# S5 preparation and scans in PSUM rings of their own, with second buffers and another order of parts

## The chip, the cores and the metric

The kernel runs on one core of one Trainium2 chip. The metric is the device time of one execution in microseconds (us). The engines are TensorE (PE; its weight loads are PEld), VectorE (DVE), ScalarE (ACT), GpSimd (POOL) and SyncE (SP), which issues all the transfers.

## The reference

One layer of a decoder trunk with two groups of heads, for 1024 new positions and 8 single tokens, in float32:

```
proj = x @ w_in                                   # q, k, v, z, two logits, u
q, k, v = short_conv(proj[qkv]);  o, S = gated_delta_chunked(q, k, v, g, beta, s0)
bu = b_bar * u;  bu[0] += lam_bar * h0            # S5: 32 groups of 16 channels, 64 complex states each
_, h = associative_scan(combine, (lam_bar, bu))   # combine = (a1*a2, a2*b1 + b2)
ys = real(c @ h) + d_skip * u
ys = gelu(ys);  ys = ys * sigmoid(ys @ w_glu + b_glu)
x = layernorm(alpha*x + concat(o, ys) @ w_out)
x = layernorm(alpha*x + relu(x @ w_ff1)**2 @ w_ff2)
```

## The kernel before

All dense products are split in a high and a low part and take three matmuls each (hi*hi, hi*lo, lo*hi). A tile of the input projection (`conv_tile`, `u_tile`) has 128 output columns: 8 slices of the 1024 inputs, three blocks of 344 positions, three matmuls each, 72 in all; its weights are loaded in two halves (`load_w`), cast by ACT (`whi`, L110) and the rest taken by POOL (`wlo`, L111). A conv tile is then evicted by ACT (L292), scaled by ACT (L300), gets three steps of the short convolution on DVE (L302) and a Silu on ACT (L303).

`run` starts with the first two u tiles beside the loads of x, then runs a list of steps, `S5O`: `uN` is a u tile, `qN`, `kN`, `vN` are conv tiles of head N, `sN` is part N of S5 (four groups of channels), `e0` the final states. Then the mixers follow, with the preparation of the GDN heads first (`gdn_prep`: transposes at L332 and L341, squares on ACT at L335, products at L357 and L358, DVE's L361 and L375). The tile framework's scheduler orders the instructions of the steps on each engine by their dependences; only from the mixers on is the order of PE written by hand.

A part of S5 (`s5_part`) has a preparation and two scans. The preparation loads `bc4`, makes small products (L925 to L932), two tables (`table`: DVE L941, POOL L942, DVE L943), of which `nat` is transposed on PE (L950) and copied to `T1` by ACT, and `V1` feeds the kt matmuls (L958); `kt` goes to the Toeplitz matrix `MT` by eight transfers (L963). Phases give `cs` and `sn` (L966 to L973). Then the carries of two pairs of groups are made by PE (L984, tile `h1`). Each pair is scanned: copies by ACT (L994), rotation by DVE (L996 to L998), two scans (L1003), copies (L1006), back rotation into `H` (L1007 to L1009). The outputs `y` are matmuls with `MT` (L1015) and `V1` (L1016); ACT copies them to `ge` (L1018), and SP stores them (L1020). `U`, `MT` and `H` have two buffers each.

PSUM has eight banks. `psum(mm, sm, ch)` opens rings of that many banks: `mmps()` takes from the first, `psm()` from the second, `pch()` from the third. In the S5 stage there are two for dense tiles and six for everything else:

```python
self.psum(2, 6)
BC, BT, BG, B3, B5 = (1, 1, 1, 2, 4)   # buffers of cs and sn, of T1, of ge; B5: of the scratch tiles t5
```

A part takes twelve banks from the ring of six, in this order: the small products, `nat`, the transposes, `V1`, kt, the phases, two `h1`, then for each pair the work bank `sb_` and `y`.

Of the kernel before, what the change touches and what calls it, by code (L numbers as in the profile page):

```python
# [11 lines left out]
AF = mybir.ActivationFunctionType  # L12
OP = mybir.AluOpType
# [12 lines left out]
RING = "XXLLLLLLQBQBQBQBQBQBQBQQCQCQQB"  # L26
FORMS = {"B11": "QL", "B21": "QL", "B12": "XX", "B22": "CL", "T1": "BQ", "T2": "BQ", "T3": "BQ", "T4": "BQ"}
TO = 2
# [18 lines left out]

LW = ((2.5, 8.25, 3.0), (3.0, 8.25, 3.0), (3.0, 8.25, 2.0), (3.0, 12.25, 3.5))
TS, MW, MF = (2, 19, 0.3)
S5O = "s0 u2 q0 s1 s2 k0 v0 u3 s3 q1 k1 v1 s4 s5 q2 k2 v2 s6 s7 e0 q3 k3"  # L50
BC, BT, BG, B3, B5 = (1, 1, 1, 2, 4)
WB = 6
WX = 1
TE = (0, 1, 2, 3)
# [4 lines left out]
class Kernel:  # L59
# [838 lines left out]
    def s5_part(self, t, du):  # L898
        nc = self.nc
# [5 lines left out]
        sb = lambda name, shape, bufs=1: sp.tile(shape, F32, name=name, tag=name, bufs=bufs)  # L905
# [11 lines left out]
        B, iB, C0, iC = (bc4[:, :, i, :] for i in range(4))  # L917
        dsk = sb("dsk", [16, 4, 16], 2)
        nc.sync.dma_start(dsk, self.a["dsk"][:, gs, :])
        tb = self.psm()[:, :128].rearrange("p (k g c) -> p k g c", g=4, c=16)  # L920
        pBb, pC0 = (tb[:, k] for k in range(2))
        Bb, iBb = sb("Bb", [128, 4, 16], 2), sb("iBb", [128, 4, 16], 2)
        w1, w2 = sb("bw1", [128, 4, 16]), sb("bw2", [128, 4, 16])
# [10 lines left out]
        sh = [128, 4, 8, 16]  # L934
        col = lambda z, a, b: z[:, gs, a:b, None].to_broadcast([128, 4, b - a, 16])
        bc = lambda z: z[:, :, None, :].to_broadcast(sh)
        bank = lambda: self.psm().rearrange("p (g k c) -> p g k c", k=8, c=16)

        def table(out, a, x, b, y, op):
            p, tm = bank(), sb("t5", sh, B5)  # L940
            V.tensor_tensor(p, a, bc(x), op=OP.mult)  # L941
            G.tensor_tensor(tm, b, bc(y), op=OP.mult)  # L942
            V.tensor_tensor(out, p, tm, op=op)  # L943

        nat = sb("t5", sh, B5)
        table(nat, col(self.prev[0], 0, 8), pBb, col(self.prev[1], 0, 8), iBb, OP.add)
        T1 = sb("T1", [128, 4, 128], BT)
        p = self.psm().rearrange("p (g m) -> p g m", m=128)
        for g in range(4):
            nc.tensor.transpose(p[:, g, :], nat[:, g].rearrange("p k c -> p (k c)"), self.ident)  # L950
        nc.scalar.activation(T1, p, AF.Copy)
        V1 = sb("V1", [128, 4, 9, 16], 2)
        nc.scalar.activation(V1[:, :, 0, :], C0, AF.Copy, scale=self.nsgn)
        table(V1[:, :, 1:9, :], col(self.lrn, 0, 8), pC0, col(self.lpi, 1, 9), iC, OP.subtract)
        kt = sp.tile([16, 4, 128], F32, name="kt", tag="t5", bufs=B5)
        p = self.psm()[:16].rearrange("p (g m) -> p g m", m=128)
        for g in range(4):
            nc.tensor.matmul(p[:, g, :], Bb[:, g, :], V1[:, g, 0:8, :].rearrange("p k c -> p (k c)"),  # L958
                             start=True, stop=True)
# [5 lines left out]
        cs3, sn3 = sb("cs", sh, BC), sb("sn", sh, BC)  # L965
        ph = sb("t5", sh, B5)  # L966
        G.tensor_tensor(ph, self.steps[:, None, :].to_broadcast(sh), self.c8[:, gs, None].to_broadcast(sh), op=OP.mult)
        p = self.psm().rearrange("p (g m) -> p g m", m=128)
        nc.scalar.activation(p, ph, AF.Identity, bias=self.magic)
        V.scalar_tensor_tensor(ph, p, -MAGIC, ph, op0=OP.add, op1=OP.subtract)  # L970
        nc.scalar.activation(sn3, ph, AF.Sin, scale=self.turn)
# [8 lines left out]
        for j in range(2):  # L980
            h1 = self.psm()
            hin.append(h1)
            for i in range(2):
                nc.tensor.matmul(h1[:, 136 * i:136 * i + 136], T1[:, 2 * j + i, :], U[:, 2 * j + i, 0:136],  # L984
                                 start=True, stop=True)
        for j in range(2):
            pr = slice(2 * j, 2 * j + 2)
            gp = slice(g0 + 2 * j, g0 + 2 * j + 2)
            h1 = hin[j][:, :272].rearrange("p (g m) -> p g m", m=136)
            sb_ = self.psm()  # L990
            sw, b = r3(sb_[:, 0:256]), r3(sb_[:, 256:512])
            b1 = sb("s5b1", [128, 2, 128], 2)
            for o, z in ((top, bot), (bot, top)):
                nc.scalar.activation(sw[o], h1[z, :, 8:136], AF.Copy)  # L994
            nc.scalar.activation(self.hinS[:, gp, :], h1[:, :, 0:8], AF.Copy)
            V.tensor_tensor(b1, h1[:, :, 8:136], cs3[:, pr, :], op=OP.mult)  # L996
            V.tensor_tensor(sw, sw, sn3[:, pr, :], op=OP.mult)
            V.tensor_tensor(b, b1, sw, op=OP.subtract)  # L998
            H = self.H[j]
            b2 = r3(hin[j][:, 0:256])  # L1000
            for i in range(2):
                g = g0 + 2 * j + i
                V.tensor_tensor_scan(b2[:, i, :], self.rho[:, g:g + 1].to_broadcast([128, 128]), b[:, i, :], 0.0,  # L1003
                                     op0=OP.mult, op1=OP.add)
            for o, z in ((top, bot), (bot, top)):
                nc.scalar.activation(sw[o], b2[z], AF.Copy)  # L1006
            V.tensor_tensor(H[:, :, 1:128], b2[:, :, 0:127], cs3[:, pr, 0:127], op=OP.mult)  # L1007
            V.tensor_tensor(sw[:, :, 0:127], sw[:, :, 0:127], sn3[:, pr, 0:127], op=OP.mult)
            V.tensor_tensor(H[:, :, 1:128], H[:, :, 1:128], sw[:, :, 0:127], op=OP.add)  # L1009
            nc.scalar.activation(self.glast[:, gp], b2[:, :, 127], AF.Copy)  # L1010
            nc.scalar.activation(H[:, :, 128:136], self.h0[:, gp, :], AF.Copy)
            y = self.psm()[:, :272].rearrange("p (g m) -> p g m", m=136)
            for i in range(2):
                g = 2 * j + i
                nc.tensor.matmul(y[:, i, :], MT[:, g, :], U[:, g, 8:144], start=True, stop=False)  # L1015
                nc.tensor.matmul(y[:, i, :], V1[:, g, 1:9, :].rearrange("p k c -> p (k c)"), H[:, i, :],  # L1016
                                 start=False, stop=True)
            nc.scalar.activation(ge[:, pr, :], y, AF.Copy)  # L1018
# [134 lines left out]
    def t_forms(self, acc, c):  # L1153
        nc = self.nc
        V, G = nc.vector, nc.gpsimd
        h = [slice(HN * j + CH * c, HN * j + CH * c + CH) for j in range(2)]
        F = {t: self.form(t, c) for t in ("T1", "T2", "T3", "T4")}
        for i in range(4):
# [3 lines left out]
            V.tensor_tensor(t[0], a12, a11, op=OP.subtract)  # L1162
            self.split_b(t[0], F["T1"][i], None, i in TP[0])
            V.tensor_tensor(t[1], a22, t[0], op=OP.subtract)
# [78 lines left out]
    def run(self):  # L1243
        nc, tc = self.nc, self.tc
# [15 lines left out]
        w = [[None, None] for _ in range(2)]  # L1260
        units = []
        w[0][0] = self.load_w(self.a["win"][16][:, 0:512])
        self.load_x(0)
        self.lam = [self._s5c(z, [128, 32], z) for z in ("aim", "ldt", "are")]
        self.lam = [self.lam[i] for i in (2, 0, 1)]
        self.setup_ba()
        w[1][0] = self.load_w(self.a["win"][17][:, 0:512])
        for k in (1, 2, 3):
            self.load_x(k)
        w[0][1] = self.load_w(self.a["win"][16][:, 512:1024])  # L1270
# [18 lines left out]
        dus = self.u_evac((0, 1), units)  # L1289
        self.ba(pss)  # L1290
        qkv = {h: [] for h in range(4)}
        self.psum(2, 6)
        for step in S5O.split():
            t = int(step[1:])
            if step[0] == "s":
# [127 lines left out]
    def bank(self):  # L1423
        return self.sb.tile([128, 1024], F32, name="sb", tag="sb")
# [28 lines left out]
    def pair(self, p):  # L1453
# [40 lines left out]
        T = bank()  # L1494
        product(T, "T1", self.form_w(s1), True)
        m5 = copy(T)
# [406 lines left out]
```

## Time and profile before

| | us |
|---|---|
| median of 3 runs | 1309.6 (1309.11 to 1309.62) |
| the profiled execution | 1303.56 |
| its span, first to last instruction | 1301.8 |
| PE busy | 1218.3 (94%) |
| DVE busy | 846.7 (65%) |
| ACT busy | 638.3 (49%) |
| POOL busy | 556.5 (43%) |

1.8 us of the profiled execution lie outside its span. Times in the trace count from the start of the span. Matmuls overlap, so that a matmul's own duration is about twice the distance from one start to the next; where work on PE is added up, distances between starts are used. The granted clock of PE is 1.00 at 2.4 GHz and 0.50 at 1.2 GHz. The S5 stage reaches from about 45 us to 256 us.

### The profile page before, as it was taken

What the parts mean: (1) busy time and instruction counts of PE and PEld (TensorE: products, weight loads), DVE (VectorE), ACT (ScalarE), POOL (GpSimd) and SP (SyncE); (2) the same over time, 40 slices, a digit from 0 to 9 for tenths busy, and PEclk for the clock granted to TensorE, in tenths of its full rate; (3) what the DMA queues carried; (4) which work ended last, traced back from release to release, by engine and by line L of the source; (5) the groups of instructions that cost most, each with busy time, mean ns of one, the idle gap of its engine ahead of it and who ended that gap; (6) DMA issues with size and microseconds to landing.
All of it is one profiled execution on the core that took longest, in us unless ns stands there. A gap on an engine that the chain in (4) does not pass through costs nothing.

```text
span 1301.8 us, 24910 instructions
## 1 busy us (share of the span) xinstructions
PE 1218.3 (94%) x9268; PEld 1186.4 (91%) x9268; DVE 846.7 (65%) x1720; ACT 638.3 (49%) x1458; POOL 556.5 (43%) x564
## 2 busy tenths in 40 slices
PE   8999998598999999989999999999899899998996
PEld 7999998488989899978999999999889898998995
DVE  6466777598546885777832323232997978778678
ACT  5366666473456752347755555555443333333200
POOL 6223343162204661544533332333657953476224
PEclk8999999599979899989999999999999999999998
DMA  7323222113441154013432232323544423334112
GB/s 213 110 58 93 65 66 80 33 16 104 131 144 34 56 171 141 1 37 115 126 123 100 105 107 98 120 100 110 164 155 126 149 91 117 121 99 155 64 40 92
DMA packets 96249, 131.14 MB, mean 101 GB/s; under 512 B 28776, under 2 KB 63992, under 8 KB 96128
## 3 DMA queue, kind: packets, MB, share of 16 engines
q1 hardware_dynamic: 96128, 129.55, 31.7%
q8 instruction: 73, 1.20, 0.4%
q14 instruction: 48, 0.39, 0.1%
HBM read 97.14 MB, written 31.20 MB: 99 GB/s over the span
## 4 chain that ended last, share of the span: by engine, by line
PE 67%; DVE 16%; issue 5%; DMA 5%; POOL 4%; ACT 3%; SPq 1%; POOLq 0%; DVEq 0%; ACTq 0%
PE sb L1438 29%; PE mm L153 7%; PE mm L155 7%; PE mm L154 7%; DMA hraw<-hd 3%; DVE t L111 2%; DVE wlo L111 1%; POOL wlo L111 1%; PE mm L1718 1%; DVE xB L1151 1%; POOL t L111 1%; PE mm L1720 1%; PE mm L1719 1%; DVE acc L1137 1%; PE mm L140 1%
## 5 line engine op out<-in xcount | busy, mean ns | idle before, releaser
L111 POOL TENSOR_TENSOR wlo<-wraw,whi 128x512 fp32r<-128x512 f32 (+1 forms) x103 | 129.5, 1260 | 174.9 <-ACT whi L110 150.7
L110 ACT ACTIVATE whi<-wraw 128x512 fp32r<-128x512 f32 (+2 forms) x194 | 113.0, 583 | 160.7 <-PE sb L1438 100.8
L1438 PE MATMUL sb<-t,whi 128*128 128x258 f32 x1008 | 163.6, 285 | 8.8 <-DVE acc L1672 8.2
L1438 PEld LDWEIGHTS sb<-t,whi 128*128 128x128 f32 x1008 | 139.8, 191 | 10.4 <-DVE acc L1672 7.0
L1438 PE MATMUL sb<-xT,whi 128*128 128x258 f32 x832 | 133.8, 283 | 0.0
L153 PE MATMUL mm<-xhi,whi 128*128 128x344 f32 x384 | 127.1, 331 | 5.2 <-DVE zt L320 4.7
L154 PE MATMUL mm<-xlo,whi 128*128 128x344 f32 x384 | 124.5, 324 | 0.0
L155 PE MATMUL mm<-xhi,wlo 128*128 128x344 f32 x384 | 124.4, 324 | 0.0
L111 DVE TENSOR_TENSOR wlo<-wraw,whi 128x512 fp32r<-128x512 f32 (+2 forms) x91 | 68.6, 755 | 71.2 <-ACT whi L110 71.1
L1438 PEld LDWEIGHTS sb<-xT,whi 128*128 128x128 f32 x832 | 114.3, 189 | 0.0
L1438 PE MATMUL sb<-t,wlo 128*128 128x258 f32 x504 | 101.5, 285 | 2.7 <-POOL wlo L111 2.2
L1438 PE MATMUL sb<-xB,whi 128*128 128x258 f32 x624 | 100.3, 283 | 0.0
L1672 DVE TENSOR_TENSOR acc<-acc,sb 128x516 f32<-128x516 f32 x112 | 75.7, 684 | 34.6 <-PE sb L1438 34.3
L1438 PEld LDWEIGHTS sb<-xB,whi 128*128 128x128 f32 x624 | 85.9, 190 | 0.0
L1438 PE MATMUL sb<-xT,wlo 128*128 128x258 f32 x416 | 83.7, 283 | 0.0
L1438 PEld LDWEIGHTS sb<-t,wlo 128*128 128x128 f32 x504 | 78.2, 190 | 3.8 <-POOL wlo L111 3.0
L153 PEld LDWEIGHTS mm<-xhi,whi 128*128 128x128 f32 x384 | 72.9, 190 | 7.3 <-DVE zt L320 5.2
L1481 DVE TENSOR_TENSOR hst<-sb,hst 128x516 f32<-128x516 f32 x40 | 27.7, 695 | 76.0 <-PE sb L1438 75.9
L155 PEld LDWEIGHTS mm<-xhi,wlo 128*128 128x128 f32 x384 | 72.9, 190 | 0.2 <-issue 0.2
L154 PEld LDWEIGHTS mm<-xlo,whi 128*128 128x128 f32 x384 | 73.0, 190 | 0.0
L1438 PEld LDWEIGHTS sb<-xT,wlo 128*128 128x128 f32 x416 | 64.1, 188 | 0.0
L1438 PE MATMUL sb<-xB,wlo 128*128 128x258 f32 x312 | 63.1, 284 | 0.0
(517 smaller groups left out, 3571.1 us busy)
## 6 DMA issues: line engine op xcount, KB each, us to landing
hraw<-hd SPq DMA_DIRECT2D x44, 516.0 KB
hd<-hst SPq DMA_DIRECT2D x52, 258.0 KB
wpair<-in_wff SPq DMA_DIRECT2D x26, 512.0 KB
w2raw<-in_wff SPq DMA_DIRECT2D x64, 192.0 KB
wraw<-in_win SPq DMA_DIRECT2D x40, 256.0 KB
wraw<-in_wff SPq DMA_DIRECT2D x24, 256.0 KB
xr<-in_xT SPq DMA_DIRECT2D x24, 172.0 KB
wraw<-in_wout SPq DMA_DIRECT2D x16, 256.0 KB
```

The lines of the kernel that those rows point to most:

```text
L110: nc.scalar.activation(hi, src, AF.Copy)
L111: (lo_eng or nc.vector).tensor_tensor(lo, src, hi.bitcast(F32), op=OP.subtract)
L140: nc.tensor.matmul(ps, hi[:, k % 4, :], mh, start=(k == 0), stop=False)
L153: nc.tensor.matmul(ps, hi[:, k % 4, :], mh, start=(k == 0), stop=False)
L154: nc.tensor.matmul(ps, hi[:, k % 4, :], ml, start=False, stop=False)
L155: nc.tensor.matmul(ps, lo[:, k % 4, :], mh, start=False, stop=(k == last))
L1137: V.scalar_tensor_tensor(x, x, self.lnp[:, 0, i:i + 1], rb, op0=OP.mult, op1=OP.mult)
L1151: nc.vector.scalar_tensor_tensor(lo, x, b, hi.bitcast(F32), op0=OP.add, op1=OP.subtract)
L1438: self.nc.tensor.matmul(ps[:, 512 * c:512 * c + CH], a[:, k, :], forms[c][k][b], start=(start and k == 0 and a is hi and b == 0), stop=(st ...
L1481: V.tensor_tensor(h3, self.banks(ps), h3, op=OP.add)
L1672: V.tensor_tensor(a, a, self.banks(ps), op=OP.add)
L1718: nc.tensor.matmul(ps, hi[:, k % 4, :], mh, start=(k == 0), stop=False)
```

## The change

In the S5 stage PSUM gets three rings: two banks for dense tiles, three for preparation (`pch`), three for scans (`psm`). The preparation's six banks come from `pch`. In the scans `y` has no bank of its own but is written into the work bank `sb_` of its pair, so that a part takes four banks from the ring of three: two `h1`, then `sb_` of each pair. `cs`, `sn`, `T1` and `ge` get a second buffer. In the code of a part the table `V1` is made ahead of the transposes of `nat`. The list of steps is another, and at the program's start the small weights `wba` and a weight load are issued ahead of three small loads. No arithmetic changes.

```diff
-S5O = "s0 u2 q0 s1 s2 k0 v0 u3 s3 q1 k1 v1 s4 s5 q2 k2 v2 s6 s7 e0 q3 k3"
-BC, BT, BG, B3, B5 = (1, 1, 1, 2, 4)
+S5O = "s0 u2 s1 q0 u3 s2 k0 s3 v0 q1 s4 k1 s5 v1 q2 s6 k2 s7 v2 e0 q3 k3"
+BC, BT, BG, B3, B5 = (2, 2, 2, 2, 4)
...
-        tb = self.psm()[:, :128].rearrange("p (k g c) -> p k g c", g=4, c=16)
+        tb = self.pch()[:, :128].rearrange("p (k g c) -> p k g c", g=4, c=16)
...
-        bank = lambda: self.psm().rearrange("p (g k c) -> p g k c", k=8, c=16)
+        bank = lambda: self.pch().rearrange("p (g k c) -> p g k c", k=8, c=16)
...
+        V1 = sb("V1", [128, 4, 9, 16], 2)
+        nc.scalar.activation(V1[:, :, 0, :], C0, AF.Copy, scale=self.nsgn)
+        table(V1[:, :, 1:9, :], col(self.lrn, 0, 8), pC0, col(self.lpi, 1, 9), iC, OP.subtract)
         T1 = sb("T1", [128, 4, 128], BT)
-        p = self.psm().rearrange("p (g m) -> p g m", m=128)
+        p = self.pch().rearrange("p (g m) -> p g m", m=128)
...
-        V1 = sb("V1", [128, 4, 9, 16], 2)
-        nc.scalar.activation(V1[:, :, 0, :], C0, AF.Copy, scale=self.nsgn)
-        table(V1[:, :, 1:9, :], col(self.lrn, 0, 8), pC0, col(self.lpi, 1, 9), iC, OP.subtract)
         kt = sp.tile([16, 4, 128], F32, name="kt", tag="t5", bufs=B5)
-        p = self.psm()[:16].rearrange("p (g m) -> p g m", m=128)
+        p = self.pch()[:16].rearrange("p (g m) -> p g m", m=128)
...
-        p = self.psm().rearrange("p (g m) -> p g m", m=128)
+        p = self.pch().rearrange("p (g m) -> p g m", m=128)
         nc.scalar.activation(p, ph, AF.Identity, bias=self.magic)
...
-            y = self.psm()[:, :272].rearrange("p (g m) -> p g m", m=136)
+            y = sb_[:, :272].rearrange("p (g m) -> p g m", m=136)
...
+        self.setup_ba()
+        w[1][0] = self.load_w(self.a["win"][17][:, 0:512])
         self.lam = [self._s5c(z, [128, 32], z) for z in ("aim", "ldt", "are")]
         self.lam = [self.lam[i] for i in (2, 0, 1)]
-        self.setup_ba()
-        w[1][0] = self.load_w(self.a["win"][17][:, 0:512])
...
-        self.psum(2, 6)
+        self.psum(2, 3, 3)
```

At the end of the S5 stage PE has, before the change, these rows one behind the other. `ps_2593` and `ps_2596` are the carries of part 6, `ps_2616` and `ps_2639` its outputs, `ps_2722` and `ps_2745` the first carry and outputs of part 7, `pc_3035` the first transposes of the GDN preparation:

```order
L984 MATMUL ps_2596<-U0_359,T1_2550 128x136 x2
L1015 MATMUL ps_2616<-U0_359,MT0_357 128x136
...
L1016 MATMUL ps_2639<-H1_356,V1_2557 128x136
L958 MATMUL ps_2694<-V1_2686,Bb_2661 16x128 x4
L984 MATMUL ps_2722<-U1_360,T1_2679 128x136 x2
...
L1015 MATMUL ps_2745<-U1_360,MT1_358 128x136
...
L1016 MATMUL ps_2768<-H1_356,V1_2686 128x136
L332 MATMUL pc_3035<-ident_186,cx_976 128x128 x4
```

With the change, the same place of PE. `ps_2611` and `ps_2614` are the carries of part 7, `ps_2412` the second outputs of part 6, `ps_2617` and `ps_2639` the outputs of part 7, `mm_2895` to `mm_2947` the three blocks of the conv tile k3, `pc_3023` the first transposes of the GDN preparation:

```order
L984 MATMUL ps_2614<-U1_360,T1_2575 128x136 x2
L1015 MATMUL ps_2412<-U0_359,MT0_357 128x136
...
L1016 MATMUL ps_2412<-H1_356,V1_2341 128x136
L153 MATMUL mm_2895<-xhi_163,whi_2889 128x344
...
L155 MATMUL mm_2947<-xhi_175,wlo_2890 128x344
L1015 MATMUL ps_2617<-U1_360,MT1_358 128x136
...
L332 MATMUL pc_3023<-ident_186,cx_1104 128x128 x4
...
L1029 MATMUL ps_2766<-glast_351,jmat_224 128x32
L1015 MATMUL ps_2639<-U1_360,MT1_358 128x136
```

The carries of part 7 moved ahead of the last outputs of part 6, 57 dense matmuls moved between these and part 7's first outputs, and part 7's second outputs moved behind the first transposes of the GDN preparation.

On ACT, at the same place, the rows ahead of the first square of the GDN preparation (L335) before the change:

```order
L1018 ACTIVATE ge_2721<-ps_2745 128x272
L1006 ACTIVATE ps_2751<-ps_2725 64x256 x2
L1010 ACTIVATE glast_351<-ps_2725 128x2
L1018 ACTIVATE ge_2721<-ps_2768 128x272
L335 ACTIVATE pt_3040,ssq_647<-pc_3035 128x128
```

and with it, where `whi_3010` and `whi_3688` are weight casts of coming tiles and `cx_2975` is the conv tile k3:

```order
L110 ACTIVATE whi_3010<-wraw_3008 128x512
L110 ACTIVATE whi_3688<-wraw_3686 128x512
L292 ACTIVATE craw_2893<-mm_2947 128x336
...
L1006 ACTIVATE ps_2639<-ps_2614 64x256
L300 ACTIVATE cx_2975<-craw_2893,wconv_196 128x1024
L1018 ACTIVATE ge_2610<-ps_2617 128x272
L1006 ACTIVATE ps_2639<-ps_2614 64x256
L1010 ACTIVATE glast_351<-ps_2614 128x2
L1018 ACTIVATE ge_2610<-ps_2639 128x272
L303 ACTIVATE cx_2975<-cx_2975 128x1024
L335 ACTIVATE pt_3028,ssq_647<-pc_3023 128x128
```

Two weight casts, an eviction and both ACT steps of the conv tile k3 moved among the last copies of part 7 and ahead of L335.

## Rows read from the trace of the kernel before

**Rows 1.** Busy time by stage: from:to and length, busy time (instructions), clock, DMA.

```profile
core 0: us, PE busy (x) PEld busy (x) DVE busy (x) ACT busy (x) POOL busy (x), PEclk, DMA share, GB/s
50.00:223.30 173.30, 172.74 (x1147) 168.92 (x1146) 114.50 (x213) 108.55 (x268) 59.63 (x69) 1.00 0.26 73
223.30:255.90 32.60, 14.70 (x65) 11.91 (x64) 22.75 (x55) 16.88 (x48) 3.83 (x4) 0.62 0.19 47
255.90:299.10 43.20, 41.31 (x305) 39.88 (x304) 35.87 (x139) 31.93 (x118) 27.74 (x51) 0.97 0.17 31
```

**Rows 2.** Timeline of PE, 223 to 256 us: start, length, what, wait before.

```profile
223.33 1.09 PE L984 MATMUL ps<-U,T 128*128 128x136 f32 x8
231.87 1.24 PE L1015 MATMUL ps<-U,MT 128*128 128x136 f32 x4 [7.45 <-DMA MT<-kt]
...
248.83 1.24 PE L1015 MATMUL ps<-U,MT 128*128 128x136 f32 x4 [6.16 <-DMA MT<-kt]
...
255.87 1.06 PE L332 MATMUL pc<-ident,cx 128*128 128x128 f32 x4
```

**Rows 3.** Timeline of PE at full clock, 200 to 222 us.

```profile
200.00 0.32 PE L153 MATMUL mm<-xhi,whi 128*128 128x344 f32 x1
...
202.84 1.09 PE L984 MATMUL ps<-U,T 128*128 128x136 f32 x8
203.68 0.41 PE L153 MATMUL mm<-xhi,whi 128*128 128x344 f32 x1
...
209.76 0.63 PE L1015 MATMUL ps<-U,MT 128*128 128x136 f32 x4
210.13 0.41 PE L155 MATMUL mm<-xhi,wlo 128*128 128x344 f32 x1
...
218.81 0.39 PE L1016 MATMUL ps<-H,V 128*128 128x136 f32 x2
...
219.41 0.41 PE L154 MATMUL mm<-xlo,whi 128*128 128x344 f32 x1
...
220.78 0.60 PE L950 MATMUL ps<-ident,t 128*128 128x128 f32 x4
221.30 1.05 PE L958 MATMUL ps<-V,Bb 128*16 128x128 f32 x8
```

**Rows 4.** Timeline of ACT in part 5, and kt matmuls in the chain of waits.

```profile
204.10 0.36 ACT L994 ACTIVATE ps<-ps 64x256 f32<-64x256 f32 x1
...
219.70 0.40 ACT L1018 ACTIVATE ge<-ps 128x272 f32<-128x272 f32 x1 [0.85 <-PE ps L1016]
...
64.99 0.98 PE ps L958 x8
...
197.57 0.98 PE ps L958 x8
```

**Rows 5.** Groups of DVE, 45 to 300 us; then its timeline at 34 and 218 us.

```profile
L926 DVE TENSOR_TENSOR bw<-fis,bc 128x64 f32<-128x64 f32 x7 | 7.8, 1121 | 0.0
...
34.58 0.22 DVE L926 TENSOR_TENSOR bw<-fis,bc 128x64 f32<-128x64 f32 x1
...
218.52 0.69 DVE L941 TENSOR_TENSOR ps<-lrn,ps 128x512 f32<-128x512 f32 x1
```

**Rows 6.** Timeline of ACT and DVE in the GDN preparation.

```profile
256.97 0.28 ACT L335 ACTIVATE pt<-pc 128x128 f32<-128x128 f32 x1 [0.46 <-PE pc L332]
...
292.35 1.15 ACT L300 ACTIVATE cx<-craw,wconv 128x1024 f32<-128x1024 f32 x1
...
299.11 1.06 ACT L303 ACTIVATE cx<-cx 128x1024 f32<-128x1024 f32 x1 [3.28 <-DVE cx L302]
...
260.05 0.29 DVE L361 SCALAR_TENSOR_TENSOR pt<-ps,ident 128x128 f32<-128x128 f32 x1 [5.20 <-ACT pt L335]
...
294.82 4.26 DVE L302 SCALAR_TENSOR_TENSOR cx<-craw,wconv,cx 128x1024 f32<-128x1024 f32 x3
```

**Rows 7.** Timeline of PE and POOL at the program's start.

```profile
10.76 1.23 PE L140 MATMUL mm<-xhi,whi 128*128 128x344 f32 x3 [3.22 <-ACT xhi L110]
...
5.86 5.44 POOL L758 TENSOR_TENSOR s5dt<-et,ldt 128x32 f32<-128x32 f32 x1 [0.24 <-DMA ldt<-in_ldt]
```

## Prediction

> **What bounds the kernel now.** I read the busy time by stage first. TensorE is busy nearly all the time except near 230 us, so the stage up to there was read more closely. From 50 to 223.3 us PE is busy 172.7 of 173.3 us at full clock (1.00, 2.4 GHz), DVE 114.5 us (66%) and ACT 108.6 us (63%) [rows 1]. From 223.3 to 255.9 us, 32.6 us, PE has only 65 matmul records, 14.7 us busy, and the granted clock is 0.62, between the two levels [rows 1]. So ahead of 223.3 the dense matmuls are the bound and hide S5; behind it they have run out, and S5 is alone on the path.
>
> The timeline of PE shows what stands in the hole [rows 2]: the carry matmuls of part 6 (L984) at 223.33, then a wait of 7.45 us for the MT transfers, its outputs, the whole of part 7 with another wait of 6.16 us for MT, and at 255.87 the first transpose of the GDN preparation (L332). No dense matmul stands between these two ends but the short remainder at 223. In the GDN preparation that follows DVE is the fuller engine: 35.9 of 43.2 us [rows 1].
>
> **What the change removes.** The parts of S5 get their PSUM from two rings and second buffers, so that part t+1's preparation runs while part t scans. By the order of PE (in the section on the change) the carry of part 7 now stands ahead of part 6's last outputs, and 57 dense matmuls stand between those and part 7's first outputs, where there was none. The number of dense matmuls is the same (942 from the e16 transposes to L332 in both). So the hole is filled, with work that stood ahead of 223.3 before, and what stays of the 32.5 us from 223.33 to 255.87 is PE's own S5 work in it, at full clock: two carries of 0.84 (202.84 to 203.68), one set of four transposes 0.52 (220.78 to 221.30), one set of kt matmuls 1.05, outputs of two parts at 0.4 for the leading pair and twice 0.6 for the rest (218.81 to 219.41), which is 1.6 a part, and the state matmul L1029, which I estimate at 0.2 as half of a short matmul pair [rows 3]. Sum 0.84 x 2 + 0.52 + 1.05 + 1.6 x 2 + 0.2 = 6.65. **Term 1: -32.54 + 6.65 = -25.9 us.**
>
> **What it moves: the handover.** In the old order the conv tiles q3 and k3 are finished in the hole. In the new one they end with the stage. Call T the end of part 6's last output on PE. PE then has 57 dense matmuls at 0.158 (18 of them from 200.00 to 202.84) [rows 3], 9.0 us, the first outputs of part 7, six dense ones, and stands at L332 at T + 10.8. On ACT, two weight casts (L110) stand ahead of the second pair's copies of part 7; they need weight slots that PE leaves only at about T + 7 and T + 9. Behind them come an eviction, k3's L300 (1.15) [rows 6] and the copy of part 7's first outputs, so the second pair's copies end near T + 12. DVE then needs L1007 to L1009 with a conv step of 1.2 to 1.3 between them (4.26 for three in the GDN stage [rows 6]), ends H at T + 15 and k3's last conv step at T + 16.6. ACT has k3's Silu (1.06) ahead of the first square of the GDN preparation (L335), and from that first square to the first L361 it took 3.1 us (256.97 to 260.05) [rows 6]. So the first L361 stands at T + 20.7, which is 9.9 us behind L332; before it was 4.2 (255.87 to 260.05) [rows 2, 6]. That is 5.7 us, of which 0.8 are outputs of part 7 that term 1 has counted already ahead of L332. **Term 2: +4.9 us.** From the first L361 on, the stage is DVE's, as before, and I take its length as unchanged. Its bounds are 0 (everything is ready when PE comes) and 9 us (the casts wait longer, and the clock falls in the wait for H).
>
> **What it adds: waits in the middle.** The scans now have three banks. In turn these are the two carries, the first pair's work bank, then the second pair's, which is the first carry's bank again. The next part's first copy (L994) waits for the second pair's outputs to be copied out, so scans of two parts can't overlap. Such a chain took 16.0 us in part 5, from its first L994 at 204.10 to the last copy of its outputs at 220.1 [rows 4], beside conv steps. The cover from one part's last outputs to the next part's is 102 to 122 dense matmuls in the new order, 107 in the mean: 107 x 0.158 + 0.84 + 0.52 + 1.05 + 1.6 = 20.9 us. If all of the DVE preparation of the next part fell on the chain (four table steps and L970 at 0.69, eight short ones at 0.22 [rows 5]), 5.2 us more, it would be 21.2: at the edge of the cover. Some of it falls into DVE's waits for ACT within the chain, so I take slack in the mean. The old order had under 0.6 us of idle PE in 173 [rows 1]. **Term 3: +1 us**, near that row; the bounds are 0 and 2 us in each of seven turns, 14 us.
>
> SP and POOL: the eight MT transfers of a part now stand beside the outputs of another part. PE's waits of 7.45 and 6.16 us for them [rows 2] came from a kt matmul with nothing behind it; the new order puts 75 dense matmuls or more, 11.9 us, between a part's kt matmuls and its outputs. A weight load queued behind them is about half a tile (36 matmuls, 5.7 us) ahead of its use. So I cost this at nothing; without that cover it would be part of term 3's upper bound. At the program's start wba and the second weight load move ahead of three small loads. PE's wait of 3.2 us there is for x [rows 7], whose load stays at the same place in SP's order, and the slow power step on POOL (5.44) [rows 7] starts about 1 us later with nobody close behind. **Term 4: 0**, bounds -1 and +1.
>
> Sum: -25.9 + 4.9 + 1 + 0 = **-20.0 us**. On the profiled execution (1303.56 us) that is 1283.6. The runs' median, 1309.6, is 6.0 above it, and the comparison is of medians: 1309.6 - 20.0 = **1289.6 us**.
>
> **The rivals.** (a) *No handover cost.* If the casts find their slots free, term 2 goes and the gain is 25 to 26 us: 1284. For it: in the hole DVE and ACT had idle time enough. Against it: k3's Silu stands ahead of L335 in ACT's order.
>
> (b) *Short waits at each pair.* DVE and POOL collide: L926 costs 1.12 us in the mean of seven, where one without POOL beside it took 0.22 [rows 5]. With preparation and scans mixed, such collisions fall on the scan chain, and 1 to 2 us in each of seven turns give 7 to 14 us back: a gain of 6 to 13, 1297 to 1304, middle 1300. The Trainium skill, "SBUF — State Buffer", section "SBUF: two separate sides", has it that DVE and GpSimd share a port pair as an exclusive lock which the loser waits for in full; by this rule the conflict is a wait of a whole POOL instruction each time, and the row on L926 agrees.
>
> (c) *The ring of three sets the pace, and it is slower.* Once a turn takes longer than its cover, PE stops at every pair's outputs. With 20 us to lose over seven turns the point is a turn of 20.9 + 20/7 = 23.8 us. Parts took 26.5 us each before (64.99 to 197.57, five of them) [rows 4]; that was PE's pace, but if it is also the chain's, the loss is 7 x (26.5 - 20.9) = 39 us less the 21 gained by terms 1 and 2: 1309.6 + 18 = 1328. Against it: the 16.0 us of part 5. The Trainium skill, "TensorE: Matmul & The Clock Gate", section "A second HAM failure mode: psum-queue depth-cycling", tells of a kernel that goes through PSUM banks in turn and whose matmul clock swings because of short stops; by that rule a loss as in this rival would be larger still, and the hole's clock of 0.62 shows that stops do lower it here, while the stage ahead of it holds 1.00.
>
> (d) *It moves nothing.* The hole stays as long because the serial steps of parts 6 and 7, not the order, make it, only beside dense work taken from elsewhere: 1309.6. Against it: in the new order the two parts' preparation is behind dense work.
>
> **How the numbers follow.** My forecast (a gain of 16 to 23) has a chance of 0.62, (a) 0.10, (b) 0.14, (c) 0.08, (d) 0.06. A change within 0.2%, 2.6 us, can't be told from none. Faster: 0.62 + 0.10 + 0.14 = 0.86; the same: 0.06; slower: 0.08. The range leaves out (c), (d) and a little of (b): from 1282 (term 1 alone, with the start's 1 us and some spread between runs) to 1303 (the upper bound of term 3 with term 2 as taken is a gain of 7).
>
> **What would show it.** Right: no stretch of 10 us at 200 to 260 us with PE under 70%; L332 near 229 us; the first L361 about 10 us behind it; no wait of PE for MT; PE busy over 97% from 50 to 225. Term 1 is wrong if dense matmuls end more than 5 us ahead of L332. Term 2 is wrong if L361 follows L332 within 6 us, or later than 14. Term 3 is wrong if PE's waits at L1015, L1016 and L984 from 60 to 220 us sum to more than 4 us. A stretch of granted clock under 0.9 ahead of 220 us would speak for (c).

## Result, and the profile after

The changed kernel takes 1290.9 us in the median (1284.3 to 1294.9, four runs) against 1309.6 of the kernel before; the ratio is 0.9849, 95% interval 0.9807 to 0.9892, so 18.7 us or 1.5% faster. In a second set of runs it was 1289.1 us, ratio 0.9851 (0.9830 to 0.9871). Predicted were 1289.6 us and a gain of 20.0. The profiled execution of the changed kernel took 1294.94 us, the longest of its four runs, while that of before was 6 us under its median; so the two traces differ by only 8.6 us, and they are compared stretch by stretch.

Busy time by stage, as in [rows 1], of the changed kernel:

```profile
core 0: us, PE busy (x) PEld busy (x) DVE busy (x) ACT busy (x) POOL busy (x), PEclk, DMA share, GB/s
...
50.00:223.30 173.30, 172.98 (x1154) 168.41 (x1154) 126.62 (x254) 114.73 (x294) 59.38 (x68) 1.00 0.28 77
223.30:255.90 32.60, 29.43 (x205) 28.08 (x204) 23.98 (x76) 23.01 (x77) 11.74 (x17) 0.95 0.15 38
255.90:299.10 43.20, 36.79 (x247) 35.21 (x246) 36.53 (x116) 23.25 (x79) 21.91 (x41) 0.96 0.28 73
```

In the stretch of the old hole PE is now busy 29.4 of 32.6 us with 205 matmul records in place of 65, at a clock of 0.95 instead of 0.62. Ahead of it DVE has 12 us more to do than before, which is S5 work that stood in the hole, and PE is still busy all the time at full clock. Its timeline at the place of [rows 2]:

```profile
221.19 0.62 PE L984 MATMUL ps<-U,T 128*128 128x136 f32 x4
221.65 0.39 PE L1015 MATMUL ps<-U,MT 128*128 128x136 f32 x2
...
222.35 0.39 PE L1016 MATMUL ps<-H,V 128*128 128x136 f32 x2
...
231.40 0.32 PE L155 MATMUL mm<-xhi,wlo 128*128 128x344 f32 x1
231.56 0.39 PE L1015 MATMUL ps<-U,MT 128*128 128x136 f32 x2
...
233.79 0.60 PE L332 MATMUL pc<-ident,cx 128*128 128x128 f32 x4
...
236.46 0.41 PE L1029 MATMUL ps<-glast,jmat 128*128 128x32 f32 x2 [1.16 <-ACT glast L1010]
238.21 0.50 PE L1015 MATMUL ps<-U,MT 128*128 128x136 f32 x2 [1.34 <-DVE H L1009]
```

Part 6's last output starts at 222.35; the dense matmuls of k3 reach to 231.4, part 7's first outputs follow at once, and L332 stands at 233.79. There is no wait for MT.

Why the preparation now runs ahead of the scans can be read on DVE. Of a part's steps, L927 is the first that writes into a PSUM bank. With six banks in turn and twelve taken by a part, this bank is that of the first carry of the part ahead, and the last steps that read that carry's bank are L1007 on DVE and L1010 on ACT. In the profile of before, part 7's L926, which feeds L927, is done at 218, but L927 stands at 231.79, right behind L1007 of part 6's first pair:

```profile
216.88 1.09 DVE L926 TENSOR_TENSOR bw<-fis,bc 128x64 f32<-128x64 f32 x1
...
231.12 0.42 DVE L1007 TENSOR_TENSOR H<-ps,cs 128x254 f32<-128x254 f32 x1 [0.81 <-ACT ps L1006]
...
231.79 0.23 DVE L927 TENSOR_TENSOR ps<-bw,bw 128x64 f32<-128x64 f32 x1
```

With the change part 7's L927 is 20.8 us ahead of that L1007:

```profile
188.82 0.22 DVE L927 TENSOR_TENSOR pc<-bw,bw 128x64 f32<-128x64 f32 x1
...
209.66 0.40 DVE L1007 TENSOR_TENSOR H<-ps,cs 128x254 f32<-128x254 f32 x1
```

This holds in every turn: L927 starts 0.7 to 2.8 us behind that L1007 in the three kernels with one ring of six (before, and a_rings and b_order of the experiments), and 9.8 to 24.0 us ahead of it in all the others.

The handover, as in [rows 6], on ACT and DVE:

```profile
233.34 1.14 ACT L300 ACTIVATE cx<-craw,wconv 128x1024 f32<-128x1024 f32 x1
...
234.93 0.36 ACT L1006 ACTIVATE ps<-ps 64x256 f32<-64x256 f32 x1
...
239.66 0.40 ACT L1018 ACTIVATE ge<-ps 128x272 f32<-128x272 f32 x1 [3.25 <-PE ps L1016]
239.95 1.05 ACT L303 ACTIVATE cx<-cx 128x1024 f32<-128x1024 f32 x1
240.90 0.27 ACT L335 ACTIVATE pt<-pc 128x128 f32<-128x128 f32 x1
...
234.59 1.28 DVE L302 SCALAR_TENSOR_TENSOR cx<-craw,wconv,cx 128x1024 f32<-128x1024 f32 x1 [1.62 <-ACT cx L300]
235.79 0.42 DVE L1007 TENSOR_TENSOR H<-ps,cs 128x254 f32<-128x254 f32 x1
...
236.45 1.28 DVE L302 SCALAR_TENSOR_TENSOR cx<-craw,wconv,cx 128x1024 f32<-128x1024 f32 x1
...
237.74 0.41 DVE L1009 TENSOR_TENSOR H<-H,ps 128x254 f32<-128x254 f32 x1
...
238.17 1.27 DVE L302 SCALAR_TENSOR_TENSOR cx<-craw,wconv,cx 128x1024 f32<-128x1024 f32 x1
...
243.38 0.29 DVE L361 SCALAR_TENSOR_TENSOR pt<-ps,ident 128x128 f32<-128x128 f32 x1 [3.83 <-ACT pt L335]
```

k3's conv steps stand between the pieces of part 7's last rotation on DVE (L302 at 234.59, 236.45 and 238.17), and its Silu (L303) ahead of the first square (L335) on ACT. The first L361 comes 9.6 us behind L332 (243.38 against 233.79), where it came 4.2 us behind it before.

From the first or last starts of lines in the traces, the stretches are, in us ("again" is the second profile of the changed kernel):

| stretch | before | after | again | predicted change |
|---|---|---|---|---|
| start to L262 | 54.6 | 58.6 | 56.8 | 0 (-1 to +1) |
| L262 to first L332 | 201.2 | 175.1 | 175.1 | -25.7 |
| first L332 to first L361 | 4.2 | 9.6 | 9.4 | +5.7 |
| first L361 to L417 (inversion loop) | 44.0 | 45.3 | 44.5 | 0 |
| L417 to the last L1800 | 993.4 | 999.8 | 998.6 | 0 |

Predicted for the second row are terms 1 and 3, less the 0.8 us of part 7's second outputs that moved behind L332. The first and the last row are the places where the two first traces differ from the prediction; the experiments take them up.

### The profile page after: what moved, and what is told of

Its sections match the earlier page's. It is cut to its first block, busy times and chain, and to the rows that moved or that the text cites. A ratio compares the mean times of both kernels' runs of the same rounds, so it can differ in the third digit from the quotient of the medians.

```text
span 1293.2 us, 24923 instructions
## 1 busy us (share of the span) xinstructions
PE 1221.9 (94%) x9268; PEld 1190.1 (92%) x9268; DVE 852.4 (66%) x1720; ACT 636.2 (49%) x1458; POOL 554.6 (43%) x564
## 4 chain that ended last, share of the span: by engine, by line
PE 67%; DVE 16%; DMA 5%; issue 4%; POOL 4%; ACT 3%; SPq 0%; POOLq 0%; DVEq 0%; ACTq 0%
PE sb L1438 31%; PE mm L153 7%; PE mm L155 7%; PE mm L154 7%; DMA hraw<-hd 2%; DVE t L111 2%; DVE wlo L111 1%; DMA xraw<-in_xT 1%; PE mm L1718 1%; DVE xB L1151 1%; PE mm L1720 1%; PE mm L1719 1%; DVE acc L1137 1%; DVE acc L1672 1%; POOL wlo L111 1%
## 5 line engine op out<-in xcount | busy, mean ns | idle before, releaser
L111 POOL TENSOR_TENSOR wlo<-wraw,whi 128x512 fp32r<-128x512 f32 (+1 forms) x103 | 131.6, 1280 | 163.3 <-ACT whi L110 143.2
L110 ACT ACTIVATE whi<-wraw 128x512 fp32r<-128x512 f32 (+2 forms) x194 | 112.9, 583 | 159.5 <-PE sb L1438 105.3
L111 DVE TENSOR_TENSOR wlo<-wraw,whi 128x512 fp32r<-128x512 f32 (+2 forms) x91 | 68.3, 752 | 71.6 <-ACT whi L110 71.3
L1672 DVE TENSOR_TENSOR acc<-acc,sb 128x516 f32<-128x516 f32 x112 | 75.7, 684 | 35.9 <-PE sb L1438 35.7
```

The source lines that it names most:

```text
L110: nc.scalar.activation(hi, src, AF.Copy)
L111: (lo_eng or nc.vector).tensor_tensor(lo, src, hi.bitcast(F32), op=OP.subtract)
L1672: V.tensor_tensor(a, a, self.banks(ps), op=OP.add)
```

## Experiments

Names that begin with a undo or alter one thing in the changed kernel, those with b add something to the kernel before. The ratio is to the kernel before on the same chip, with its 95% interval. The last column is the time from L262 to the first L417 in the kernel's one profile; it leaves out the start and the unchanged rest, and is 249.4 us in the kernel before and 230.1 in the first profile of the changed kernel.

| kernel | rings | list | second buffers | median us | ratio | L262 to L417, us |
|---|---|---|---|---|---|---|
| changed, again | 2,3,3 | new | yes | 1289.1 | 0.9851 (0.9830 to 0.9871) | 229.1 |
| a_start | 2,3,3 | new | yes | 1287.4 | 0.9847 (0.9828 to 0.9867) | 229.6 |
| a_bufs | 2,3,3 | new | no | 1287.7 | 0.9843 (0.9825 to 0.9861) | 230.3 |
| a_rings | 2,6 | new | yes | 1317.9 | 1.0074 (1.0055 to 1.0094) | 257.4 |
| a_order | 2,3,3 | old | yes | 1297.2 | 0.9915 (0.9891 to 0.9939) | 237.3 |
| b_rings | 2,3,3 | old | no | 1296.6 | 0.9916 (0.9896 to 0.9936) | 236.3 |
| b_order | 2,6 | new | no | 1317.0 | 1.0068 (1.0048 to 1.0088) | 257.8 |
| br_order | 2,3,3 | new | no | 1290.7 | 0.9866 (0.9847 to 0.9885) | 227.5 |
| a_242 | 2,4,2 | new | yes | 1286.0 | 0.9824 (0.9809 to 0.9838) | 230.7 |
| a_242 again | 2,4,2 | new | yes | 1286.9 | 0.9831 (0.9813 to 0.9850) | 229.7 |
| a_y | 2,3,3, y apart | new | yes | 1286.4 | 0.9833 (0.9809 to 0.9857) | 228.6 |
| a_nok3 | 2,3,3 | new | yes | 1285.9 | 0.9825 (0.9811 to 0.9840) | 226.2 |

### The program's start undone (a_start)

```diff
-        self.setup_ba()
-        w[1][0] = self.load_w(self.a["win"][17][:, 0:512])
         self.lam = [self._s5c(z, [128, 32], z) for z in ("aim", "ldt", "are")]
         self.lam = [self.lam[i] for i in (2, 0, 1)]
+        self.setup_ba()
+        w[1][0] = self.load_w(self.a["win"][17][:, 0:512])
```

> The changed kernel with the old order of the loads at the program's start. Theory (the new start order costs time): in the changed kernel PE waited 2.65 us for a weight cast (L140 at 29.80), had a granted clock of 0.66 from 30 to 35 us, and was 4.0 us late at L262 (58.6 against 54.6 us). With the old order that wait is gone, L262 stands near 54.6 us and the median falls by 4, from 1290.9 to about 1287. Rival (the 4 us are a matter of one execution, not of the order): L262 in either place, the median at 1290.9 as before, give or take 2.

L262 stood at 56.9 us, not 54.6. The median, 1287.4, is the one that the theory named, but the kernel before took 1308.1 us beside it, and the ratio, 0.9847, is that of the changed kernel. The wait at 29.80 in the changed kernel's first profile differs from execution to execution:

```profile
29.80 0.42 PE L140 MATMUL ps<-xhi,whi 128*128 128x344 f32 x1 [2.65 <-ACT whi L110]
```

The same wait was 2.2 us in b_rings and 1.4 us here, both with the old start, 0.8 us in the changed kernel's second profile, and none in that of before and in one of a_242. L262 stood at 54.6, 56.9, 55.5, 54.9 and 56.2 us in the five profiles with the old start (mean 55.6), and from 54.6 to 58.6 in the nine with the new one (mean 56.4). Of the 4.0 us of the first profile 1.5 are a fall of the clock behind L229, which the last section tells of; the other 2.5 stand already at L229 (47.76 against 45.28). My theory fell; the rival holds in its main point, that most of the 4 us belongs to one execution. The new order of loads costs at most a microsecond, and these runs can't tell that from nothing.

### The old rings (a_rings)

```diff
-        tb = self.pch()[:, :128].rearrange("p (k g c) -> p k g c", g=4, c=16)
+        tb = self.psm()[:, :128].rearrange("p (k g c) -> p k g c", g=4, c=16)
...
-            y = sb_[:, :272].rearrange("p (g m) -> p g m", m=136)
+            y = self.psm()[:, :272].rearrange("p (g m) -> p g m", m=136)
...
-        self.psum(2, 3, 3)
+        self.psum(2, 6)
```

> The changed kernel with the old two rings in the S5 stage (two banks for dense tiles, six for all else, y in a bank of its own); new list of steps, second buffers and new start stay. Theory (the split of the rings is what lets the preparation of a part run beside the scans of the part ahead): the order of PE has the second outputs of part 6 and the whole of part 7 behind the last dense matmul again, so a hole of 20 to 30 us with PE under half busy stands ahead of L332, L332 is back near 255 us, and the median is 1305 to 1316, above 1309 if the 4 us of the start stay. Rival 1 (the list of steps or the second buffers carry the gain): no such hole, 1289 to 1296.

1317.9 us, slower than the kernel before: the hole is back, and longer. L332 stands at 264.5 us, where 255 was expected, and the median is 2 us above the expected range. The waits of PE from 45 to 290 us (in total, times, longest), the first rows:

```profile
PE ps L1015 <- DMA MT<-kt: 11.3, 2, 6.1
PE ps L953 <- DVE t L943: 7.0, 2, 5.1
PE ps L1029 <- ACT glast L1010: 1.9, 1, 1.9
```

Part 7 again goes through its steps one by one, with waits for MT as in [rows 2], and now part 6 waits for its table as well (L943 ahead of L953). So without the rings the rest of the change gains nothing and costs 9.8 us.

### Rings alone (b_rings), and the list undone (a_order)

b_rings is the kernel before with the three rings and `y` in `sb_`. a_order is the changed kernel with one line turned back:

```diff
-S5O = "s0 u2 s1 q0 u3 s2 k0 s3 v0 q1 s4 k1 s5 v1 q2 s6 k2 s7 v2 e0 q3 k3"
+S5O = "s0 u2 q0 s1 s2 k0 v0 u3 s3 q1 k1 v1 s4 s5 q2 k2 v2 s6 s7 e0 q3 k3"
```

> The kernel before with the three rings (2, 3, 3) and y in its work bank alone; old list of steps, single buffers, old start. Theory (the rings alone close the hole): the carries of part 7 stand ahead of the second outputs of part 6 and PE has dense matmuls up to L332, which stands near 230 us; L361 follows some 9 us behind. The cover of parts 1 and 2 is short in this list (62 and 64 dense matmuls, 10 us), so some waits of 1 to 3 us there. Median 1287 to 1295; without the 4 us of the start as likely under the changed kernel's 1290.9 as over it. Rival 1 (the list of steps or the second buffers are needed): parts wait for cs, sn and T1 of the part ahead, PE stands still 1 to 3 us in each of seven turns, 1300 to 1310.

> The changed kernel with the old list of steps; rings, second buffers, V1 ahead of the transposes and the new start stay. Theory (with the rings in place the list is worth some 8 us, because it lets the last part finish with dense matmuls still beside it): a wait of PE of several us for part 7's copies near the end, L361 some 4 us later than in the changed kernel (243.4 us), median 1293 to 1299, as with the rings alone (1296.6). Rival (second buffers, V1 or the start make up the 8 us): 1286 to 1291.

They agree: 0.9916 and 0.9915. The rings alone give 11 to 12 us, about three fifths of the gain (13.1 us of 19.3 to 20.3 from L262 to L417), and second buffers, `V1` and the start add nothing to them. What is missing shows at the end of the stage, in the timeline of PE of b_rings:

```profile
237.53 0.79 PE L1015 MATMUL ps<-U,MT 128*128 128x136 f32 x2 [6.37 <-ACT ps L994]
...
241.83 0.64 PE L1029 MATMUL ps<-glast,jmat 128*128 128x32 f32 x2 [2.15 <-ACT glast L1010]
```

a_order has the same waits, 6.4 and 2.2 us. With the old list part 7's kt matmuls (the last L958) stand at 214.1 us, where they were at 206.6 in the changed kernel, because more dense tiles stand ahead of the late parts; L332 comes at 229.7, so that the dense work has ended before part 7 has scanned its first pair. The expectation for b_rings was 1287 to 1295 with short waits in parts 1 and 2; PE had no wait there (0.2 us in all from 60 to 220 us), and it missed the one at the end: L361 follows L332 by 17.8 us, where 9 was expected.

### The list alone (b_order), and rings with list (br_order)

> The kernel before with the new list of steps alone; old rings, single buffers, old start. Theory (the list helps only where the rings let it): by the order of PE the dense matmuls run out behind part 6's first outputs, so the hole ahead of L332 is there as before, L332 near 255 to 262 us, and the median is 1306 to 1316. Rival 1 (the list carries a share by itself, about 8 us, the difference between the kernel with the rings alone, 1296.6, and the changed kernel without second buffers, 1287.7): 1298 to 1302.

> The kernel before with the three rings, y in the work bank and the new list of steps; single buffers, V1 behind the transposes and the old start stay. Theory (rings and list together are the whole change): by the order of PE the parts' last outputs stand as in the changed kernel up to the last six dense matmuls; 1286 to 1291, within 3 us of the changed kernel of this call. Rival (V1, second buffers or the start are needed too, as one package with the list): 1293 to 1297, as with the rings alone (1296.6).

The list alone makes the kernel before slower by 7 to 9 us (1.0068), a little beyond what was expected. By the order of PE, part 6 stands behind the last dense matmul from its transposes (L950) on, where before it was from its carries on. The timeline of PE of b_order, and the end of its hole:

```profile
226.56 1.11 PE L950 MATMUL ps<-ident,t 128*128 128x128 f32 x4 [5.30 <-DVE t L943]
...
238.42 1.25 PE L1015 MATMUL ps<-U,MT 128*128 128x136 f32 x4 [5.48 <-DMA MT<-kt]
...
256.30 1.25 PE L1015 MATMUL ps<-U,MT 128*128 128x136 f32 x4 [5.92 <-DMA MT<-kt]
...
263.35 1.06 PE L332 MATMUL pc<-ident,cx 128*128 128x128 f32 x4
```

Together, in br_order, rings and list give 0.9866, within 2 us of the changed kernel measured beside it, and the intervals overlap. So the two edits don't add: the list is worth +7 to +9 us without the rings and some -6.5 us with them (ratio 0.9916 to 0.9866). The stretch from L262 to L417, in single profiles, says the same: +8.4 us without the rings (249.4 to 257.8), -8.8 with them (236.3 to 227.5).

### Single buffers (a_bufs)

```diff
-BC, BT, BG, B3, B5 = (2, 2, 2, 2, 4)
+BC, BT, BG, B3, B5 = (1, 1, 1, 2, 4)
```

> The changed kernel with one buffer each for cs, sn, T1 and ge. Theory (the rings carry the gain, and by the order of PE the carries stand at nearly the same places among the dense matmuls): 1290 to 1295, waits of PE at L984, L1015 and L1016 from 60 to 220 us up to 4 us in all. Rival 2 (without second buffers the next part's phases and T1 wait for the scans ahead): waits of 1 to 3 us in each of seven turns, 1298 to 1310.

0.9843, no different from the changed kernel; the median, 1287.7, is 2 us under the expected range. From 60 to 220 us PE was busy 159.2 of 160.0 us. The second buffers of `cs`, `sn`, `T1` and `ge` bring nothing that can be measured here.

### The handover (a_nok3)

```diff
-        for j in (1, 2, 3):
+        for j in (1, 2, 3) if t != 7 else ():
             nc.vector.scalar_tensor_tensor(out, raw[:, j:j + NP], cw[:, t, j:j + 1], out, op0=OP.mult, op1=OP.add)
-        nc.scalar.activation(out, out, AF.Silu)
+        if t != 7:
+            nc.scalar.activation(out, out, AF.Silu)
```

> The changed kernel without the three steps of the short convolution on DVE (L302) and the Silu (L303) of the conv tile k3; this part of the computation is left out. Theory (term 2: k3's steps in the middle of part 7's last rotation delay the handover): the last L1009 stands at 236.1 in place of 237.7 us, the Silu of 1.05 us ahead of L335 is gone, and the first L361 follows L332 by 7.0 us in place of 9.6; the median is 2 to 4 us under the changed kernel's: 1284 to 1288.5. Rival (part 7's scan itself sets the handover, and DVE has room for k3): L361 stays 9 to 9.6 us behind L332, the median within 1 us of 1288 to 1291.

The timeline of DVE (line numbers are one higher behind this edit, so L362 is L361):

```profile
231.53 0.42 DVE L1008 TENSOR_TENSOR H<-ps,cs 128x254 f32<-128x254 f32 x1 [2.35 <-ACT ps L1007]
...
232.32 0.42 DVE L1010 TENSOR_TENSOR H<-H,ps 128x254 f32<-128x254 f32 x1
...
236.85 0.29 DVE L362 SCALAR_TENSOR_TENSOR pt<-ps,ident 128x128 f32<-128x128 f32 x1 [3.78 <-ACT pt L336]
```

The last piece of H is written in one go behind the copies, and the first L361 follows L332 (230.0) by 6.9 us instead of 9.6; 7.0 was expected. So k3's steps cost 2.5 to 2.7 us of the handover, as term 2 says. The other half of its growth stays without them: 6.9 us is still 2.7 more than the 4.2 of before. The first square (L335) stands 4.4 us behind L332 there, where it was 1.1 before; ACT copies part 7's second outputs (L1018) ahead of it, and these wait for the last H. From L262 to L417 it is 2.9 to 3.9 us less than in the two profiles of the changed kernel, more than the handover, since 3.8 us of DVE work is left out of a stretch in which DVE is the fuller engine. The ratio, 0.9825, is 3.4 us under that of the changed kernel's second set of runs (0.9851), but the two intervals overlap, so the medians alone don't show it.

### Four banks for scans (a_242), and y in a bank of its own (a_y)

```diff
-        self.psum(2, 3, 3)
+        self.psum(2, 4, 2)
```

> The changed kernel with four banks for the scans and two for the preparation, in place of three and three. By the order of PE the parts then stand 71 to 108 dense matmuls apart, and 86 dense matmuls stand behind part 7's last outputs. Theory (a part's chain of 16 us fits into the shorter cover when the scans of two parts may overlap, and a dense end hides part 7): PE doesn't wait at L1029 and L1015 near the end (1.2 and 1.3 us in the changed kernel), only k3's conv steps stand ahead of L335, L361 follows L332 by 5 to 8 us in place of 9.6, median 1283 to 1288. Rival (the chain sets the pace: cover of the first parts is 15.2 to 16.8 us against a chain of 16): PE waits 2 to 5 us at L1015 or L984 in each of three or four turns, 1293 to 1302.

> The changed kernel with four banks for scans and two for preparation, once more, beside the changed kernel on one chip. Theory (a dense end hides part 7 and the handover, but DVE, which is the fuller engine of the GDN preparation, takes most of it back: from L229 to the start of the inversion loop, L417, it took 241.6 us, the changed kernel 240.9): 0 to 3 us under the changed kernel of this call. Rival (the whole handover of some 5 us is won): 4 to 6 us under it.

Here S5 ends early: the last outputs are at 221.0 us, 86 dense matmuls follow, and in the timelines of PE and DVE stand

```profile
236.33 0.60 PE L332 MATMUL pc<-ident,cx 128*128 128x128 f32 x4
...
239.45 0.29 DVE L361 SCALAR_TENSOR_TENSOR pt<-ps,ident 128x128 f32<-128x128 f32 x1 [0.40 <-ACT pt L335]
...
240.12 1.27 DVE L302 SCALAR_TENSOR_TENSOR cx<-craw,wconv,cx 128x1024 f32<-128x1024 f32 x1
```

L361 comes 3.1 us behind L332, better than expected, and no wait of PE for the scans is left from 60 to 223 us (its 2.2 us of waits are for evictions and one weight part), although two parts' last outputs are copied as near as 13.3 us to each other (L1018 at 110.3 and 123.6). But from the first L361 to L417 it took 47.8 us, 3 more than in the changed kernel's second profile. k3's last conv step (1.27 us) falls into this stretch; DVE is busy 39.1 us in it instead of 37.3, ACT 35.9 instead of 32.5, and which of them sets the 3 us isn't shown. From L229 to L417 the first profile has 241.6 us and the second 239.1, but 1.5 us of this difference is the fall of the clock ahead of L262, which only the first has. From L262 it is 230.7 and 229.7 us, where the changed kernel has 230.1 and 229.1. So what the handover wins is given back, and the traces have no gain. The medians are 2.2 to 4.9 us under the changed kernel's, but the intervals of 0.9831 and 0.9851 overlap widely: it is not shown to be faster.

```diff
-            y = sb_[:, :272].rearrange("p (g m) -> p g m", m=136)
+            y = self.psm()[:, :272].rearrange("p (g m) -> p g m", m=136)
```

> The changed kernel with y in a bank of its own from the ring of three again, so that a part takes six scan banks instead of four. Theory (the ring of three has slack: covers of 100 dense matmuls against a chain of 16 us): by the order of PE the first outputs of a part move up to 40 dense matmuls nearer to the last ones of the part ahead and its carries move behind these; PE waits under 4 us in all at L984, L1015 and L1016, and the median is 0 to 6 us over the changed kernel of this call. Rival (c) of the prediction (the ring of three sets the pace): waits of 2 to 4 us in each of seven turns, 1302 to 1316.

a_y takes six scan banks a part from the ring of three, and is as fast: 0.9833, 1286.4 beside 1289.1 us, with overlapping intervals, where up to 6 us more was expected. Its only wait of PE from 60 to 230 us:

```profile
PE mm L155 <- POOL wlo L111: 0.3, 1, 0.3
```

So that `y` shares the work bank isn't needed, and the ring of three isn't the bound.

## Why the prediction was right

**Term 1, the hole (-25.9), and term 3, waits in the middle (+1).** Together with the 0.8 us of outputs they made -25.7 from L262 to L332; measured was -26.1 in both profiles. Its steps can be seen: no dense matmul is lost (942 in each of the two), PE has no wait for MT, k3's last dense matmul starts 2.4 us ahead of L332 and six more stand right ahead of it, and PE is busy 173.0 of 173.3 us from 50 to 223.3. That the rings make it is shown by a_rings and br_order and by the place of L927; the prediction named second buffers beside them, and a_bufs shows that these aren't needed. PE's waits from 60 to 223 us come to 0.3 us, so term 3 was nearly zero, at the lower end of its bounds. A turn took 21.3 us in the mean (last L1018 of parts 0 and 6 at 95.1 and 222.8, six turns), where the cover was worked out as 20.9.

**Term 2, the handover (+4.9).** Part 6's last output ends at T = 222.5, where the next dense matmul starts. L332 was forecast at T + 10.8 and came at T + 11.3; the second pair's copies at T + 12 and T + 12.8; H at T + 15 and T + 15.7; k3's last conv step at T + 16.6 and T + 16.9; the first L361 at T + 20.7 and T + 20.9. From L332 to L361 +5.7 was forecast and +5.4 and +5.2 measured. a_nok3 shows that half of it is made by k3's steps; the other half is part 7's last scan, which ends behind L332.

One step of this path was not as told. The weight casts on ACT (L110) stood at T + 7.2 and T + 9.2, as forecast, but the second pair's copies (L1006) didn't wait for them. The first copy waited another 0.38 us for DVE's second scan (L1003), in rows of the first profile of the changed kernel, of ACT and then of DVE:

```profile
229.70 0.63 ACT L110 ACTIVATE whi<-wraw 128x512 fp32r<-128x512 f32 x1 [0.34 <-PE mm L154]
231.65 0.63 ACT L110 ACTIVATE whi<-wraw 128x512 fp32r<-128x512 f32 x1 [1.32 <-PE mm L154]
...
233.06 0.36 ACT L1006 ACTIVATE ps<-ps 64x256 f32<-64x256 f32 x1 [0.38 <-DVE ps L1003]
...
230.64 1.35 DVE L1040 TENSOR_TENSOR ssmw<-lpi,ih 128x256 f32<-128x256 f32 x1
...
232.56 0.41 DVE L1003 TENSOR_TENSOR_SCAN ps<-rho,ps 128x128 f32<-128x128 f32 x1
```

Ahead of that scan DVE had steps of the final states (`e0`), one of which, L1040, took 1.35 us beside POOL's L111 (230.42 to 231.70), where it took 0.42 before. The second copy stood behind k3's L300 and the copy of the first outputs, as forecast. So the time of the copies came out partly by luck, while k3's steps behind them are as told. What I took as unchanged behind it, L361 to L417, grew by 0.5 to 1.4 us.

**Term 4, the start (0).** The first trace has +4.0 us at L262, outside my bounds of -1 and +1, which is also why L332 stands at 233.8 and not near 229. The means over all profiles, 55.6 with the old start and 56.4 with the new one, show that most of it is a matter of the execution, so the term stands, but its bounds are too narrow for a single trace.

**The sum.** From L262 to L417, where the change acts, the changed kernel took 230.1 and 229.1 us against 249.4 before: -19.3 and -20.3, where -20.0 was forecast. A part of this agreement is chance: the +1 of term 3 wasn't there, and the growth between L361 and L417, which the sum didn't have, stands in its place. Behind L417 nothing was changed, and the stretch to the end took 993 to 1003 us over the profiles of all these kernels, 993.4 in the one profile of before and 999.8 in the first of the changed kernel. These 6.3 us and the 4.0 us at the start are why two single traces differ by 8.6 us where the medians differ by 18.7 and 19.7. Putting the gain on the median, not on the profiled execution, was what the number needed.

**The rivals.** (a) no handover cost: L361 came 9.6 us behind L332. Its condition, casts that find their slots free, would not have been enough, since the copies didn't wait for the casts. (b) short waits by collisions: PE's waits were 0.3 us, and L926, 1.12 us in the mean before [rows 5], became shorter, as the group of DVE from 45 to 300 us shows:

```profile
L926 DVE TENSOR_TENSOR bw<-fis,bc 128x64 f32<-128x64 f32 x7 | 4.7, 674 | 0.0
```

The Trainium skill, "SBUF — State Buffer", section "SBUF: two separate sides", has DVE and GpSimd hold their shared ports in turn. The traces agree: before, each of the seven started up to 0.1 us behind a POOL instruction (L942 or L111) and ended within 0.1 us of its end, after 1.08 to 1.33 us. With the change only three did so (1.10), two met the last part of an L942 (0.49 and 0.50), and two met none (0.21). So such collisions are real, but L926 has fewer of them; one that fell on a scan, that of L1040, cost 0.9 us. (c) the ring of three as the pace: a turn of 21.3 us is under the 23.8 that this rival needs, PE held a granted clock of 1.00 from 60 to 220 us, and a_y, which takes half as many banks again from the same ring, is no slower. (d) nothing moves: the hole is filled.

What the prediction did not have is how the edits depend on each other. It argued from the whole order of PE, which was enough for the number, but it would not have told that the rings alone give three fifths, that the list alone loses, and that the second buffers, `V1`, the start and `y` in `sb_` bring nothing that can be measured.

## What to carry to other kernels

When a helper stage runs beside a bound engine, its first and last parts are where its serial steps show; a pool that preparation and use share can force them into one sequence, because the next part's first buffer is one that the part ahead still uses; a pool of its own for each lets the preparation run ahead. Whether the bound engine's work then reaches to the end of the stage is a matter of the order of the parts too: here the pools alone gave three fifths. Read in the new order of the bound engine how much of its work stands between the last steps of the helper, and multiply by the distance between starts from the trace: here that gave the change from L262 to L332 to half a microsecond. Test such edits in combination, since one that gains behind another can lose alone.

## What was not expected of the hardware

Behind the 16 small matmuls at L228 (1.95 us, 16x8 each) the granted clock falls from 1.00 to 0.50 for about 3 us in some executions of a program and not in others; nine of the fourteen profiles here have it. Two profiles of a_242, the windows around it, the first profile:

```profile
40.00:46.00 6.00, 6.00 (x44) 4.47 (x44) 0.06 (x1) 4.35 (x11) 2.57 (x2) 1.00 0.77 262
46.00:50.00 4.00, 4.00 (x17) 4.00 (x17) 3.43 (x21) 0.59 (x3) 0.10 (x1) 0.57 0.35 91
50.00:54.00 4.00, 4.00 (x27) 4.00 (x27) 0.74 (x4) 0.46 (x1) 0.00 (x0) 1.00 0.19 51
```

and the second:

```profile
40.00:46.00 6.00, 6.00 (x44) 4.47 (x44) 0.55 (x6) 3.88 (x9) 2.18 (x3) 1.00 0.82 278
46.00:50.00 4.00, 4.00 (x27) 4.00 (x26) 3.36 (x19) 1.05 (x4) 0.00 (x0) 1.00 0.34 91
```

From 40 to 46 us the two have the same 44 matmul records at full clock; then one has 17 and the other 27 in 4 us. It costs 1.5 us: from L229 to L262 it is 10.9 us with the fall and 9.4 without. What decides it stays open.
